# Raw input transposed first, and copies given to whichever engine is free: a two-block transformer kernel on one core

## Chip, cores and metric

The kernel runs on one core of a Trainium2 chip. It computes the forward pass of two transformer blocks for one sequence of 256 tokens of width 1024, everything in float32. The metric is the device time of one execution in microseconds, taken as the median of three executions. The kernel before takes 878.27 us (878.02 to 880.94).

## What is computed

`x` is 256 x 1024. The first block normalises it, multiplies it with `w_in` (and, later, with the four merge gates), runs four kinds of attention on the pieces, merges them and adds a feed-forward layer with a short convolution; the second block has two more mixers, a cross attention and another feed-forward layer. The change touches the first lines of this, which in the reference are:

```python
def rms_norm(x, gain):
    y = x * lax.rsqrt(jnp.mean(x * x, axis=-1, keepdims=True) + 1e-6)
    return y * gain
...
h = rms_norm(x, norm_attn_pre)        # 256 x 1024
p = h @ w_in                          # split into latent, key, value and gate columns
g = sigmoid(h @ w_merge_gate[j])      # four of them
```

The norm's factor is one number per token, so `(r * (x * gain)) @ w` equals `r * ((x * gain) @ w)`: it may be multiplied in on either side of the product.

## The kernel before

**Products.** Each float32 operand is split in two rounded parts, `hi` and `lo`, and a product is three TensorE products (hi times hi, hi times lo, lo times hi) that add up in one PSUM bank. `W` (line 439) does it for weights: a DMA into one of three `raw` buffers, a cast to `hi` on ScalarE (`S.copy`), a subtraction to `lo` on VectorE (`V.tensor_sub`). Activations are kept transposed: `XT` (line 457) holds, for each of eight slices of 128 of the 1024 inner columns, the `hi` and `lo` part of a 128 x 256 tile. `lin` (line 557) keeps activations stationary and streams up to 512 weight columns; `linT` (line 584) keeps weights stationary and streams 512 columns (both halves of the activation) or 256 (one half), by turns. There are 82 calls of `linT`, with sixteen products each.

**The start.** `mats1` (line 680) loads `x` in four pieces of 128 x 512 into `xs[0]` and `xs[1]` (`tt` is the half of 128 tokens), the first panel `wi0` of 432 columns in four pieces, and a constant table. For each half it forms the mean square (a square on ScalarE for one 512 columns, a square with sum on VectorE for the other), raises it to the power -0.5 on GpSimd, multiplies `x` by the factor on VectorE (line 711), and only then transposes it on TensorE (line 714) in eight pieces of 128 x 128. Each piece is copied out of PSUM with the gain, `hi` by ScalarE (`S.mul`, line 718) and `lo` by VectorE (line 719). The first product follows, `wi0`; its results go through `evac0`.

**The order of work.** No instruction is issued where it is written. `Plan` (line 21) records all of them, with what each reads and writes, and `trial` (line 160) plays them through with a cost per instruction (`_Op`, line 325): each engine takes, when it is free, the ready instruction with the lowest priority number for which a buffer is free. `hurry` (line 271) brings forward what TensorE waited for in the trial, and `issue` (line 291) keeps the best of 40 such rounds. The queues are then issued in that order, so the engines run their instructions strictly one after the other in an order fixed beforehand. Every instruction has a fixed engine: `S` is ScalarE, `V` VectorE, `G` GpSimd, `PE` TensorE; the author chose, line by line, which copies ScalarE makes and which VectorE.

**Places named later.** `attend` (line 646) computes two heads of an attention: scores, exponentials on ScalarE, four multiplications by the reciprocal sum, transposes by `transP` (line 628), values. `make_ffn` (line 1195) is the feed-forward layer: `natural` steps use `lin` and transpose the result back, `stationary` steps use `linT` and add the halves, `S.copy(u, acc[:, 0])` (line 1224). Since all instructions are issued from the recording layer, the profile shows them with line 101; the names of the tiles tell them apart: `bank` is a PSUM bank, `raw`, `hi`, `lo` the weights, `x` the activations in two parts and the input, `k` work tiles, `sm` small columns, `junk` a target that nobody reads, `ident` the identity matrix of the transposes.

## Time and profile before

| | us |
|---|---|
| median of three executions | 878.27 |
| the profiled execution | 878.73 |
| its span | 877.0 |
| TensorE busy | 858.2 |
| VectorE busy | 639.8 |
| ScalarE busy | 490.9 |
| GpSimd busy | 47.3 |

The profile shows one execution. The span runs from the first instruction to the last; 1.73 us of the execution's time lie outside it. A matmul's busy time is longer than the distance to the next one, because matmuls are pipelined: how fast TensorE goes is read from the distances between starts, not from the durations.

### The profile page before, as it was taken

How to read it: one execution, taken by the hardware profiler on the slowest of the kernel's cores; microseconds unless marked ns; L12 is line 12 of the kernel's file. 1: busy time of each engine (PE TensorE's matmuls, PEld its weight loads, DVE VectorE, ACT ScalarE, POOL GpSimd, SP SyncE). 2: the span in 40 equal slices, each digit the busy share in tenths (PEclk: the TensorE clock that was granted, in tenths of full speed). 3: DMA queues.
4: the chain of work that ended last, by engine and by line, in shares of the span. 5: the costliest groups of instructions: out<-in, count | busy, mean ns of one | idle time of the engine just before them, and what ended most of it. 6: DMA issues, size and time to landing. Idle time of an engine off the chain costs nothing.

```text
span 877.0 us, 12151 instructions
## 1 busy us (share of the span) xinstructions
PE 858.2 (98%) x4436; PEld 715.8 (82%) x4436; DVE 639.8 (73%) x1148; ACT 490.9 (56%) x845; POOL 47.3 (5%) x58
## 2 busy tenths in 40 slices
PE   6999999999999999999999999999999999999997
PEld 5779886778887888888888887788888888888886
DVE  6885648976667988888978677967855677666662
ACT  5675535654455667666654457656644555545441
POOL 1200000000001000000010111201100000000000
PEclk9999999999999999999999999999999999999999
DMA  7646653577456567665636564455633566656541
GB/s 246 213 148 201 210 178 97 178 215 220 133 175 218 171 212 223 207 194 180 205 131 201 173 191 146 144 169 168 202 111 97 186 201 215 213 182 200 182 134 49
DMA packets 45186, 156.08 MB, mean 178 GB/s; under 512 B 5263, under 2 KB 6841, under 8 KB 44997
## 3 DMA queue, kind: packets, MB, share of 16 engines
q1 hardware_dynamic: 44228, 153.10, 55.6%
q0 software_dynamic: 896, 2.19, 0.9%
q8 instruction: 35, 0.57, 0.3%
q14 instruction: 27, 0.21, 0.1%
HBM read 154.21 MB, written 1.06 MB: 177 GB/s over the span
## 4 chain that ended last, share of the span: by engine, by line
PE 82%; DVE 7%; ACT 4%; issue 2%; DMA 2%; POOL 1%; SPq 0%; DVEq 0%; POOLq 0%; ACTq 0%
PE bank L101 82%; DVE k L101 3%; ACT k L101 2%; DVE lo L101 2%; ACT hi L101 1%; DVE x L101 1%; POOL sm L101 1%; DMA raw<-in_fdn 1%; DVE sm L101 1%; DMA raw<-in_xkv 1%; DMA raw<-in_wi 1%; ACT junk L101 0%; ACT L101 0%; SPq L101 0%; ACT x L101 0%
## 5 line engine op out<-in xcount | busy, mean ns | idle before, releaser
L101 PE MATMUL bank<-hi,x 128*128 128x512 f32 (+3 forms) x1556 | 494.8, 393 | 2.0 <-ACT x L101 1.0
L101 DVE TENSOR_TENSOR lo<-raw,hi 128x1024 fp32r<-128x1024 f32 (+2 forms) x279 | 334.8, 1209 | 93.1 <-ACT hi L101 91.0
L101 ACT CAST hi<-raw 128x1024 fp32r<-128x1024 f32 (+2 forms) x279 | 287.6, 1039 | 102.0 <-PE bank L101 48.9
L101 PEld LDWEIGHTS bank<-hi,x 128*128 128x128 f32 (+1 forms) x1556 | 290.4, 188 | 60.1 <-DVE x L101 2.8
L101 PE MATMUL bank<-lo,x 128*128 128x512 f32 (+3 forms) x786 | 307.6, 393 | 0.1
L101 PE MATMUL bank<-x,hi 128*128 128x512 f32 x656 | 228.5, 398 | 0.0
L101 PE MATMUL bank<-x,lo 128*128 128x256 f32 x656 | 170.9, 281 | 0.0
L101 PEld LDWEIGHTS bank<-lo,x 128*128 128x128 f32 (+1 forms) x786 | 147.3, 187 | 28.5 <-DVE lo L101 0.8
L101 PEld LDWEIGHTS bank<-x,hi 128*128 128x128 f32 x656 | 119.0, 188 | 22.8
L101 PEld LDWEIGHTS bank<-x,lo 128*128 128x128 f32 x656 | 123.8, 189 | 7.6
L101 ACT COPY k<-bank 128x256 f32<-128x256 f32 (+5 forms) x116 | 46.1, 399 | 91.9 <-PE bank L101 91.6
L101 PE MATMUL bank<-ident,k 128*128 128x128 f32 (+2 forms) x362 | 58.5, 278 | 11.4 <-DVE k L101 9.8
L101 PEld LDWEIGHTS bank<-ident,k 128*128 128x128 f32 (+2 forms) x362 | 44.2, 140 | 25.1 <-DVE k L101 15.6
L101 POOL TENSOR_TENSOR sm<-sm,nhalf 128x1 f32<-128x1 f32 (+3 forms) x36 | 37.6, 1046 | 500.4 <-DVE sm L101 457.5
L101 DVE TENSOR_TENSOR x<-bank,x 128x512 fp32r<-128x512 f32 (+4 forms) x62 | 36.3, 608 | 28.3 <-PE bank L101 21.1
L101 DVE TENSOR_TENSOR k<-k,bank 128x256 f32<-128x256 f32 (+1 forms) x78 | 32.6, 419 | 26.4 <-ACT k L101 25.6
L101 PE MATMUL bank<-k,k 64*128 64x256 f32 (+12 forms) x364 | 49.0, 325 | 0.7 <-DVE k L101 0.7
L101 ACT ACTIVATE k<-bank 128x512 f32<-128x512 f32 (+4 forms) x41 | 19.7, 483 | 49.9 <-PE bank L101 47.7
L101 PEld LDWEIGHTS bank<-k,k 64*128 64x128 f32 (+4 forms) x364 | 37.7, 176 | 10.8 <-issue 4.1
L101 ACT ACTIVATE k<-bank,sm 128x256 f32<-128x256 f32 (+1 forms) x42 | 22.6, 566 | 27.4 <-PE bank L101 19.9
L101 DVE SCALAR_TENSOR_TENSOR k<-k,convw,k 128x255 f32<-128x255 f32 x72 | 34.4, 480 | 4.1 <-ACT k L101 3.4
L101 ACT CAST x<-bank 128x512 fp32r<-128x512 f32 (+2 forms) x49 | 24.4, 515 | 17.9 <-PE bank L101 17.2
(97 smaller groups left out, 404.7 us busy)
## 6 DMA issues: line engine op xcount, KB each, us to landing
raw<-in_wi SPq DMA_DIRECT2D x42, 512.0 KB, 4.4
raw<-in_up SPq DMA_DIRECT2D x40, 512.0 KB, 4.2
raw<-in_fup SPq DMA_DIRECT2D x36, 512.0 KB, 4.3
raw<-in_wg SPq DMA_DIRECT2D x32, 512.0 KB, 4.3
raw<-in_fdn SPq DMA_DIRECT2D x22, 512.0 KB, 4.6
raw<-in_dn SPq DMA_DIRECT2D x22, 512.0 KB, 4.6
raw<-in_xkv SPq DMA_DIRECT2D x16, 512.0 KB, 4.1
raw<-in_wo SPq DMA_DIRECT2D x8, 512.0 KB, 4.3
```

The lines of the kernel that those rows point to most:

```text
L101: op = _Op(self, n, eng, lambda: getattr(target, name)(*map(self.place, a), **{x: self.place(y) for x, y in k.items()}), name, outs, ins, k)
```

## The change

It has four parts.

1. The input goes to TensorE as it arrives. The transposes read `x` itself (`turn_in`), and the copies out of PSUM multiply with the gain alone. The gain is loaded as eight rows and transposed on TensorE, in place of a column load. The norm's factor is computed beside this and kept in spare columns of `nhalf` (`rx`, with `rq8` and `rhalf` as its multiples); it is multiplied in where results of products with `h` leave PSUM, mostly as the scalar of a copy that was there before. For `wi5`, whose results lie transposed, it is needed along the row: two products of a matrix of ones with a diagonal matrix make `rT`, and six multiplications apply it. Six products of ones are issued at the very start, into a bank that nobody reads. The first piece of `wi0` comes in two halves, the second half of `x` behind the second piece, and the constant table after that. The products of `wi0` for both token halves run side by side in two banks.
2. `nc.any`, here `AN`, records a copy or a scaling with two ways, one for VectorE and one for ScalarE. `trial` puts it in both queues and the engine that comes to it first takes it. Copies of transposes, of attention outputs, of the feed-forward's halves and the scalings in `attend` use it.
3. `issue` makes 120 rounds, and `hurry` sometimes pushes what a later product waits for.
4. `linT` first runs seven products with `hi`, then the eight with `lo`, then the last with `hi`.

The convolution's weights move from a tile of their own to a work buffer. The core of the diff:

```diff
@@ -106,6 +107,11 @@
             op = old
         elif self.gluing:
             self.glued = op
+        if other:
+            e2, t2, n2, a2, k2 = other
+            alt = _Op(self, n, e2, lambda: getattr(t2, n2)(*map(self.place, a2), **k2), n2, outs, ins, k2)
+            op.ways = {eng: (op.cost, op.parts), e2: (alt.cost, alt.parts)}
+            op.eng = "ANY"
         op.urgent = self.urgent
         op.prio = n - self.urgent * self.URGE - (0 if self.bulk else self.bonus) if self.at is None or name != "dma_start" else self.at
...
 
     reserve = {"k4": 1, "x8": 2, "k2": 3, "x2": 2, "k1": 2, "sm": 4, "PS": 2}
 
@@ -369,6 +394,20 @@
         return lambda *a, **k: self._p.add(self._e, self._t, name, a, k)
 
 
+class _Any:
+
+
+    def __init__(self, plan, nc):
+        self._p, self._nc = plan, nc
+
+    def copy(self, o, a):
+        self._p.add("DVE", self._nc.vector, "tensor_copy", (o, a), {}, ("ACT", self._nc.scalar, "copy", (o, a), {}))
+
+    def scale(self, o, a, c):
+        self._p.add("DVE", self._nc.vector, "tensor_scalar", (o, a, c, None), {"op0": OP.mult},
+                    ("ACT", self._nc.scalar, "mul", (o, a, c), {}))
+
+
 def tile_two_blocks(tc, T, out, dbg=None):
...
@@ -589,13 +629,11 @@
         h3 = hi.rearrange("p (k n) -> p k n", k=8)
         l3 = lo.rearrange("p (k n) -> p k n", k=8)
         plan.bulk = True
+        for kt in range(7):
+            PE.matmul(acc.rearrange("p a t -> p (a t)"), h3[:, kt], xt.both(kt), start=kt == 0, stop=False)
         for kt in range(8):
-            low = lambda: PE.matmul(acc[:, 0], l3[:, kt], xt.sl(kt, 0, 256)[0], start=False, stop=False)
-            if kt == 7:
-                low()
-            PE.matmul(acc.rearrange("p a t -> p (a t)"), h3[:, kt], xt.both(kt), start=kt == 0, stop=kt == 7)
-            if kt < 7:
-                low()
+            PE.matmul(acc[:, 0], l3[:, kt], xt.sl(kt, 0, 256)[0], start=False, stop=False)
+        PE.matmul(acc.rearrange("p a t -> p (a t)"), h3[:, 7], xt.both(7), start=False, stop=True)
         plan.bulk = False
         return acc
...
@@ -625,13 +663,13 @@
...
-    def transP(s, eng):
+    def transP(s):
...
         pT = sb([128, 384], "k2", name="pT")
-        eng(pT, ps)
+        AN.copy(pT, ps)
         return pT
...
         for u in range(2):
             for tt in (1, 0):
-                V.tensor_scalar(ss[u][:, COLS[tt]], ss[u][:, COLS[tt]], rec[:, 2 * tt + u:2 * tt + u + 1], None, op0=OP.mult)
-        pts = [transP(s, (V.tensor_copy, S.copy)[u]) for u, s in enumerate(ss)]
+                AN.scale(ss[u][:, COLS[tt]], ss[u][:, COLS[tt]], rec[:, 2 * tt + u:2 * tt + u + 1])
+        pts = [transP(s) for s in ss]
         values(po, pts, vs, first, last)
 
     def outT(oT, i, po):
-        S.copy(oT[0][:, i], po)
+        AN.copy(oT[0][:, i], po)
         V.tensor_sub(oT[1][:, i], po, f(oT[0][:, i]))
...
@@ -691,72 +729,113 @@
     plan = g["plan"]
     plan.at = -4000
-    for i in range(2):
-        nc.sync.dma_start(xs[0][:, i * 512:(i + 1) * 512], T["x"][:128, i * 512:(i + 1) * 512])
+    plan.urgent = True
+    ones = keep([128, 128], "ones")
+    V.memset(ones, 1.0)
+    warm = psS([128, 128])
+    for i in range(6):
+        PE.matmul(warm, ones, ones, start=True, stop=True)
+    h = XT(8)
+    chunks = two(T["wi0"])
+    first = []
...
+    def turn_in(tt, i):
+        tp = psS([128, 4, 128])
+        for j in range(4):
+            PE.transpose(tp[:, j, :], xs[tt][:, i * 512 + j * 128:i * 512 + (j + 1) * 128], ident)
+        for j in range(4):
+            k = 4 * i + j
+            hh, hl = h.sl(k, tt * 128, tt * 128 + 128)
+            S.mul(hh, tp[:, j, :], gcol[:, k:k + 1])
+            V.scalar_tensor_tensor(hl, tp[:, j, :], gcol[:, k:k + 1], f(hh), op0=OP.mult, op1=OP.subtract)
+
+    grow = sb([8, 128], "k1", name="grow")
+    nc.scalar.dma_start(grow, T["grow"])
+    load(0)
...
+    gp = psS([128, 8])
+    PE.transpose(gp, grow, ident[:8, :8])
+    V.tensor_copy(gcol, gp)
+    turn_in(0, 0)
+    first = [(W(chunks[0][0][:, j * 432:(j + 1) * 432], 432), 1) for j in range(2)]
+    turn_in(0, 1)
+    first.append((W(chunks[1][0], 864), 2))
+    load(1)
+    turn_in(1, 0)
+    first.append((W(chunks[2][0], 864), 2))
+    turn_in(1, 1)
+    first.append((W(chunks[3][0], 864), 2))
...
+    rcol = g["nhalf"][:, 8:14].rearrange("p (t c) -> p t c", t=2)
+    rx, rq8, rhalf = ([rcol[:, tt, i:i + 1] for tt in range(2)] for i in range(3))
...
     for tt in range(2):
-        r = g["rs2"](g["halves"](xs[tt], True))
-        for i in range(2):
...
-                PE.transpose(tp[:, j, :], xn[:, j * 128:(j + 1) * 128], ident)
-            for j in range(4):
-                k = 4 * i + j
-                hh, hl = h.sl(k, tt * 128, tt * 128 + 128)
-                S.mul(hh, tp[:, j, :], gcol[:, k:k + 1])
-                V.scalar_tensor_tensor(hl, tp[:, j, :], gcol[:, k:k + 1], f(hh), op0=OP.mult, op1=OP.subtract)
+        V.tensor_copy(rx[tt], g["rs2"](g["halves"](xs[tt], True)))
+        V.tensor_scalar(rq8[tt], rx[tt], -0.125, None, op0=OP.mult)
+        V.tensor_scalar(rhalf[tt], rx[tt], 0.5, None, op0=OP.mult)
+        V.tensor_scalar(dg[tt], ident, rx[tt], None, op0=OP.mult)
+        PE.matmul(rrow[:, tt * 128:tt * 128 + 128], ones, dg[tt], start=True, stop=True)
+    V.tensor_copy(rT, rrow)
 
     latg = sb([128, 384], "k2", name="latg")
...
+        S.mul(q[:, :, :64], a[:, 0], rq8[tt])
+        V.tensor_scalar(k[:, :, :64], a[:, 1], rx[tt], None, op0=OP.mult)
         cum = cps[:, tt, :]
         V.tensor_scalar(q[:, :, 64], cum, -1.0, None, op0=OP.mult)
...
     for c in range(6):
         acc = linT(h, T["wi5"][c], psA)
+        t = sb([128, 256], "k1", name="bqk")
         if c < 3:
-            t = sb([128, 256], "k1", name="bqs")
             S.mul(t, acc[:, 0], -0.125)
-            V.scalar_tensor_tensor(bq[:, c], acc[:, 1], -0.125, t, op0=OP.mult, op1=OP.add)
+            V.scalar_tensor_tensor(t, acc[:, 1], -0.125, t, op0=OP.mult, op1=OP.add)
         else:
-            t = sb([128, 256], "k1", name="bks")
             S.copy(t, acc[:, 0])
-            V.tensor_add(bk[:, c - 3], acc[:, 1], t)
-
+            V.tensor_add(t, acc[:, 1], t)
+        V.tensor_mul((bq if c < 3 else bk)[:, c % 3], t, rT)
 
     mg = [sb([128, 2, 512], "k4", name="merged") for _ in range(2)]
...
                 nat = sb([128, 512], "k2", name="nat")
-                S.copy(nat[:, :256], acc[:, :256])
-                V.tensor_copy(nat[:, 256:], acc[:, 256:])
+                AN.copy(nat[:, :256], acc[:, :256])
+                AN.copy(nat[:, 256:], acc[:, 256:])
                 u = us[c // 2][:, c % 2]
-                S.copy(u, acc[:, 0])
+                AN.copy(u, acc[:, 0])
                 V.tensor_add(u, u, acc[:, 1])
```

What the order becomes is shown at three places. ScalarE at the start, before: `x0` and `x1` are the halves of the input, `raw0` to `raw2` the pieces of `wi0`, `x80` and `x81` the transposed activations, `bank` tiles the transposes.

```order
L101 ACTIVATE junk0_133,sm1_120<-x0_150 128x512
L101 CAST hi0_66<-raw0_63 128x864
L101 CAST hi1_67<-raw1_64 128x864
L101 ACTIVATE x80_90<-bank0_135,sm0_119 128x128 x2
L101 CAST hi2_68<-raw2_65 128x864
L101 ACTIVATE x80_90<-bank0_135,sm0_119 128x128 x2
L101 ACTIVATE x81_91<-bank1_136,sm0_119 128x128 x4
L101 ACTIVATE junk0_133,sm3_122<-x1_151 128x512
L101 CAST hi3_69<-raw0_63 128x864
L101 CAST hi4_70<-raw1_64 128x1024
L101 ACTIVATE x80_90<-bank3_138,sm0_119 128x128 x4
L101 ACTIVATE x81_91<-bank4_139,sm0_119 128x128 x4
```

and now:

```order
L102 ACTIVATE junk0_133,sm1_120<-x0_150 128x512
L102 ACTIVATE x80_90<-bank2_137,sm0_119 128x128 x3
L102 CAST hi0_66<-raw0_63 128x432
L102 ACTIVATE x80_90<-bank2_137,sm0_119 128x128
L102 CAST hi1_67<-raw1_64 128x432
L102 ACTIVATE x81_91<-bank3_138,sm0_119 128x128 x4
L102 CAST hi2_68<-raw2_65 128x864
L102 ACTIVATE junk0_133,sm4_123<-x1_151 128x512
L102 ACTIVATE x80_90<-bank5_140,sm0_119 128x128 x4
L102 ACTIVATE x81_91<-bank6_141,sm0_119 128x128 x4
L102 CAST hi3_69<-raw0_63 128x864
L102 CAST hi4_70<-raw1_64 128x864
```

The gain copies of the first half (`x80`, `x81`) stand ahead of the first casts where they stood behind two of them, and the casts of half pieces (128x432) between them; no factor is waited for.

TensorE at the start, before (`k26`, `k27` are the normalised input):

```order
L101 MATMUL bank0_135<-ident_143,k26_100 128x128 x4
L101 MATMUL bank1_136<-ident_143,k27_101 128x128 x4
L101 MATMUL bank2_137<-hi0_66,x80_90 128x432
L101 MATMUL bank2_137<-lo0_74,x80_90 128x432
L101 MATMUL bank2_137<-hi0_66,x80_90 128x432 x2
L101 MATMUL bank2_137<-lo0_74,x80_90 128x432
L101 MATMUL bank2_137<-hi0_66,x80_90 128x432
L101 MATMUL bank2_137<-hi1_67,x80_90 128x432
```

and now:

```order
L102 MATMUL bank0_135<-ones_152 128x128 x6
L102 MATMUL bank1_136<-ident_143,k10_110 128x8
L102 MATMUL bank2_137<-ident_143,x0_150 128x128 x4
L102 MATMUL bank3_138<-ident_143,x0_150 128x128 x4
L102 MATMUL bank4_139<-hi0_66,x80_90 128x432
L102 MATMUL bank4_139<-lo0_74,x80_90 128x432
L102 MATMUL bank4_139<-hi0_66,x80_90 128x432
L102 MATMUL bank4_139<-hi1_67,x80_90 128x432
L102 MATMUL bank4_139<-lo1_75,x80_90 128x432
L102 MATMUL bank4_139<-hi1_67,x80_90 128x432
L102 MATMUL bank5_140<-ident_143,x1_151 128x128 x4
L102 MATMUL bank4_139<-hi2_68,x80_90 128x432
```

Ahead of the transposes stand six products of ones and the transpose of the gain; the transposes read `x0`, and those of the second half follow the products of the first two inner slices.

ScalarE at the first two up steps of the first feed-forward layer, before (`convw` is the convolution's weights, `k27` a result on its way to TensorE's transposes):

```order
L101 COPY k26_100<-bank7_142 128x256
L101 CAST hi2_68<-raw1_64 128x1024
L101 ACTIVATE k22_96<-bank4_139,convw_154 128x256 x2
L101 ACTIVATE k23_97<-bank0_135,convw_154 128x256 x2
L101 COPY k27_101<-bank1_136 128x256
L101 CAST hi6_72<-raw2_65 128x1024
```

and now (`k10` holds the convolution's weights; `k25`, `k20` belong to the first step, `k26` to the second):

```order
L112 COPY k25_99<-bank1_136 128x256 x2
L102 CAST hi0_66<-raw2_65 128x1024
L102 CAST hi3_69<-raw0_63 128x1024
L102 CAST hi2_68<-raw1_64 128x1024
L112 COPY k20_94<-bank3_138 128x256
L102 CAST hi5_71<-raw2_65 128x1024
L102 ACTIVATE k24_98<-bank5_140,k10_110 128x256 x2
L102 ACTIVATE k21_95<-bank4_139,k10_110 128x256 x2
L112 COPY k26_100<-bank7_142 128x256 x2
L102 CAST hi1_67<-raw0_63 128x1024
```

The copies of the first step are now shared with VectorE; the copy for the second step, now both halves of it, still stands behind four convolution instructions.

## Rows read from the trace of the kernel before

**Rows 1.** The page's first part: busy us, share, instructions.
```profile
PE 858.2 (98%) x4436; PEld 715.8 (82%) x4436; DVE 639.8 (73%) x1148; ACT 490.9 (56%) x845; POOL 47.3 (5%) x58
```

**Rows 2.** By stretch: busy (instructions) of PE, PEld, DVE, ACT, POOL; PEclk, DMA.
```profile
7.08:17.20 10.12, 8.64 (x24) 6.64 (x25) 7.78 (x17) 7.37 (x15) 2.32 (x4) 1.00 0.82 275
17.20:25.80 8.60, 8.60 (x47) 7.74 (x46) 6.50 (x22) 6.00 (x17) 1.11 (x2) 1.00 0.59 156
285.00:450.00 165.00, 165.00 (x863) 140.48 (x863) 144.03 (x225) 107.31 (x169) 1.54 (x2) 1.00 0.60 188
```

**Rows 3.** Timeline of the first 14 us: start, duration, instruction [idle before <-releaser].
```profile
3.68 0.63 ACT L101 ACTIVATE junk<-x 128x512 bf16<-128x512 f32 x1 [1.66 <-DMA x<-in_x]
7.08 1.97 PE L101 MATMUL bank<-ident,k 128*128 128x128 f32 x8 [7.08 <-DVE k L101]
10.00 0.73 PE L101 MATMUL bank<-hi,x 128*128 128x432 f32 x1 [0.96 <-ACT x L101]
13.10 1.09 PE L101 MATMUL bank<-hi,x 128*128 128x432 f32 x2 [0.52 <-DVE x L101]
```

**Rows 4.** Timeline, 14 to 26 us: the first product and the second half's transposes.
```profile
15.43 0.92 PE L101 MATMUL bank<-hi,x 128*128 128x432 f32 x2
16.51 0.92 PE L101 MATMUL bank<-hi,x 128*128 128x432 f32 x2
17.92 1.04 PE L101 MATMUL bank<-ident,k 128*128 128x128 f32 x8
18.56 2.17 ACT L101 ACTIVATE x<-bank,sm 128x128 fp32r<-128x128 f32 x8 [2.48 <-PE bank L101]
22.04 0.56 PE L101 MATMUL bank<-hi,x 128*128 128x432 f32 x2
22.63 0.55 PE L101 MATMUL bank<-hi,x 128*128 128x432 f32 x2
25.37 0.59 PE L101 MATMUL bank<-hi,x 128*128 128x432 f32 x2
```

**Rows 5.** ScalarE's groups by shape: count | busy us, mean ns | idle before.
```profile
L101 ACT COPY k<-bank 128x256 f32<-128x256 f32 x91 | 33.7, 371 | 76.6 <-PE bank L101 76.4
L101 ACT ACTIVATE junk<-x 128x512 bf16<-128x512 f32 x18 | 11.4, 632 | 30.1 <-DVE x L101 28.4 <-DMA x<-in_x 1.7
L101 ACT CAST hi<-raw 128x864 fp32r<-128x864 f32 x4 | 3.7, 916 | 3.5 <-DMA raw<-in_wi 3.5
```

**Rows 6.** VectorE's groups by shape.
```profile
L101 DVE COPY k<-bank 128x256 f32<-128x256 f32 x10 | 4.2, 422 | 3.6 <-ACT k L101 2.5 <-PE bank L101 1.0
L101 DVE TENSOR_TENSOR lo<-raw,hi 128x864 fp32r<-128x864 f32 x4 | 4.2, 1054 | 1.2 <-ACT hi L101 1.2
L101 DVE TENSOR_SCALAR k<-k,sm 128x256 f32<-128x256 f32 x34 | 11.7, 349 | 0.4
L101 DVE SCALAR_TENSOR_TENSOR x<-bank,sm,x 128x128 fp32r<-128x128 f32 x16 | 4.6, 344 | 2.0 <-ACT x L101 2.0
```

**Rows 7.** Timeline, 330 to 333 us: TensorE in two calls of linT.
```profile
331.95 0.40 PE L101 MATMUL bank<-x,hi 128*128 128x512 f32 x1
332.18 0.28 PE L101 MATMUL bank<-x,lo 128*128 128x256 f32 x1
332.30 0.40 PE L101 MATMUL bank<-x,hi 128*128 128x512 f32 x1
```

**Rows 8.** TensorE's waits: waited for: us in total, times, longest us.
```profile
PE bank L101 <- DVE k L101: 10.5, 9, 7.1
PE bank L101 <- ACT k L101: 1.3, 1, 1.3
```

**Rows 9.** Timeline, 281 to 285 us: the second up step's copy.
```profile
282.29 1.93 ACT L101 ACTIVATE k<-bank,convw 128x256 f32<-128x256 f32 x4
284.53 0.44 PE L101 MATMUL bank<-ident,k 128*128 128x128 f32 x2 [1.26 <-ACT k L101]
```

More of the change, by code (lines that the diff above doesn't have):

```diff
@@ L195, in trial @@
                 _, n = heapq.heappop(pend)
-                heapq.heappush(heaps[ops[n].eng], (prio[n], n))
+                for e in ("DVE", "ACT") if ops[n].eng == "ANY" else (ops[n].eng,):
+                    heapq.heappush(heaps[e], (prio[n], n))
+                    look[e] = True
             while rel and rel[0][0] <= t:
@@ L247, in trial @@
                 else:
-                    end = tfree[e] = t + o.cost
+                    end = tfree[e] = t + cost
                 done += 1
@@ L693, in mats1 @@
     plan.at = -4000
-    for i in range(2):
-        nc.sync.dma_start(xs[0][:, i * 512:(i + 1) * 512], T["x"][:128, i * 512:(i + 1) * 512])
-    gcol = small(8)
-    nc.sync.dma_start(gcol, T["gcol"])
-    first = two(T["wi0"])
-    for i in range(3):
-        first[i] = (W(first[i][0], 864), 2)
-    for i in range(2):
-        nc.sync.dma_start(xs[1][:, i * 512:(i + 1) * 512], T["x"][128:, i * 512:(i + 1) * 512])
-    first[3] = (W(first[3][0], 864), 2)
-    nc.sync.dma_start(g["cst"], T["cst"])
@@ new lines, in mats1, with load @@
+    ones = keep([128, 128], "ones")
[6 more added lines that the diff above has]
+    first = []
+    def load(tt):
+        for i in range(2):
+            c = slice(i * 512, (i + 1) * 512)
+            nc.sync.dma_start(xs[tt][:, c], T["x"][tt * 128:tt * 128 + 128, c])
+    def turn_in(tt, i):
[7 more added lines that the diff above has]
+            V.scalar_tensor_tensor(hl, tp[:, j, :], gcol[:, k:k + 1], f(hh), op0=OP.mult, op1=OP.subtract)
@@ L755, in evac0 @@
         hh = lat[0][:, :, tt * 128:(tt + 1) * 128]
-        S.copy(hh, tp)
+        AN.copy(hh, tp)
         V.tensor_sub(lat[1][:, :, tt * 128:(tt + 1) * 128], tp, f(hh))
-    lin(h, [(first, 432)], evac0)
+    accs = [psA([128, 432]) for _ in range(2)]
+    kt = 0
+    plan.bulk = True
+    for (hi, lo), kc in first:
+        h3, l3 = (w.rearrange("p (k n) -> p k n", k=kc) for w in (hi, lo))
+        for j in range(kc):
+            for tt in range(2):
+                mm3(accs[tt], *h.sl(kt, tt * 128, tt * 128 + 128), h3[:, j], l3[:, j], kt == 0, kt == 7)
+            kt += 1
+    plan.bulk = False
+    nc.sync.dma_start(g["cst"], T["cst"])
+    for tt in range(2):
+        evac0(0, tt, accs[tt])
     tab = sb([36, 16], "sm", name="tab")
@@ L860, in mats1 @@
                 PE.transpose(tp[:96, i, :], src[:, i, :], ident)
[L861 to L864 removed]
+            AN.copy(dst[:96, :, c0:c1], tp[:96])
     oTs = {}
@@ L1326, in trans4 @@
         if scale is None:
-            S.copy(d, tp)
+            AN.copy(d, tp)
         else:
```

135 lines of the change are left out of this document (73 added, 62 removed).

## The prediction

> **What bounds the kernel now.** The page's busy times come first: TensorE is busy for 858.2 of 877.0 us [rows 1], so the kernel is almost a single row of products, and an edit is worth only what it takes from TensorE's row or from the places where that row stands still. I then read TensorE's waits by cause [rows 8]. The named ones come to 10.5 + 1.3 = 11.8 us. One of them is 7.1 us, and the timeline shows that it is the start: the first eight transposes begin at 7.08, released by VectorE's normalised input, although the first half of `x` was there at 3.68, when ScalarE's square began [rows 3]. That leaves 11.8 - 7.1 = 4.7 us for all other named waits, in some ten places; the longest is 1.26 us, at the second up step of the first feed-forward layer, where a copy stands behind four convolution instructions on ScalarE [rows 9].
>
> The rest of the start is read from distances between products. The first product begins at 10.00; from 13.10 they follow without pause [rows 3]. From 15.43 to 16.51 three products start, 0.36 us each; from 22.04 to 22.63 three more, 0.197 each [rows 4]. The same 432 columns are streamed, so the early pace is that of 1.2 GHz and the late one that of 2.4, although the granted clock is printed as 1.00 in both stretches [rows 2]. The eight transposes tell the same: 1.97 us at 7.08, 1.04 us at 17.92 [rows 3, 4]. The change lies between 16.51 and 17.92. The last product of `wi0` ends at about 25.8; three products of `wi1` and two other transposes (0.9 us) were done between, so the net mark of the start is **24.9**. The same mark in the changed kernel gives the gain of the start.
>
> **The start in the changed kernel.** The transposes read `x`, so they go at 3.7 and fill the first bank after four at 0.25 us, at 4.7. What was waited for before, square, power and scaling, leaves the path. Next late is ScalarE, whose order the change section shows. After its square (3.68 + 0.63 [rows 3, 5] and the reading of its sum, so about 4.6) it has sixteen gain copies at 2.17/8 = 0.27 us [rows 4], together 4.35; two casts of half pieces at about 0.47 (half of the 0.916 [rows 5], an estimate), 0.94; three casts at 0.916, 2.75; and the second square, 0.8 with its sum. That is 8.85 us and ends at 13.5 to 14.0, if no load comes late. VectorE's two splits of the last pieces take 1.05 each [rows 6], the first from 13.1, so that the last `lo` is there at 15.2 to 15.6. Some twelve products stand behind that: 12 x 0.197 = 2.4.
>
> What TensorE does with this depends on its clock. Up to 12.5 it is limited by ScalarE's and VectorE's data: some 14 of the 48 products can have been done, 34 remain. At the fast pace from there the last data decide: 15.6 + 2.4 + two diagonal products at 0.13 to 0.25 (nearest: the transposes [rows 3, 4]) gives 18.4, a gain of 6.5. If the clock rises at 17.2, as now, 13 more products go by then at 0.36, and 21 at 0.197 take 4.1: 21.5, a gain of 3.4. At the slow pace throughout it would be 12.5 + 34 x 0.36 = 24.7, a gain of 0.2. I take a rise at about 15, because the row of products without pause, which now begins at 13.10, begins some 2 us earlier: 7 products by 15, then 27 x 0.197 = 5.3, so 20.3, and with the diagonal products 20.2 to 20.6. **The gain of the start is 4.5**, between 0.2 and 6.5.
>
> The six products of ones lie in the 3.7 us in which TensorE has nothing (6 x 0.25 = 1.5 us); they cost nothing, and whether they raise the clock is the difference between the cases above. The transpose of the gain stands ahead of the first transposes on TensorE: should the eight rows land after `x`, every transpose behind it waits, one for one. The diagonal products and the ready factor are not waited for before the results of `wi0` leave PSUM. Behind that, the products of `wi1` cover the additional multiplication of the two latent factors.
>
> **The factor at the exits.** Most of these multiplications are the scalar of a copy that is there anyway: nothing. The six with `rT` are new on VectorE, about 0.42 each by the copy of the same size [rows 6], 2.5 us, beside TensorE's products of `wi5` and the gates. Four scalings of the input (128 x 512) go. On the sum: 0.
>
> **`linT`.** The sixteen products stay, seven with `hi` in a row instead of by turns. A `hi` product takes 0.23 until the next start, a `lo` one 0.12 [rows 7], 8 x 0.35 = 2.8 us a call either way. If the order among them changed a distance by 0.01 us, 82 calls would make 82 x 0.01 = 0.8 either way. I take 0.
>
> **Copies by either engine, and more rounds.** By the new order VectorE has 26 more copies of 128 x 256, ScalarE as many fewer, 25 attention scalings went the other way, and eight `ah` scalings went to VectorE. A copy is dearer on VectorE, 0.422 against 0.371 [rows 5, 6]: 26 x 0.05 = 1.3 us more work, off the path. The Trainium skill ("VectorE: DVE Perf Modes", Specifications) states that VectorE lies closer to SBUF and ScalarE closer to PSUM, which speaks against moving copies out of PSUM to VectorE; the two rows agree with it, by 0.05 us a copy, and by it the sum stays as it is while VectorE has time to spare. What this part can win is bounded by the 4.7 us of named waits (with the small ones between them, little more); what it can lose has no row, so I set the same 4.7 on the other side. The longest wait seems to stay: in the new order both copies of the second up step still stand behind four convolution instructions on ScalarE, and then 1.26 + 0.37 could be waited for. I take **+2.0**, under half of the bound.
>
> **The sum.** 4.5 + 2.0 = 6.5. The profiled execution took 878.73, span 877.0 and 1.73 beside it; the median is 0.46 lower. Taken from the median: 878.27 - 6.5 = **871.8 us**.
>
> **The rivals.** A gain or loss of 0.5%, 4.4 us, is about what can be told from no change here, so "faster" is under 873.9 and "slower" over 882.7.
>
> *The clock rises no earlier and the copies win nothing.* Speaking for it: at present the eight transposes and sixteen products up to 17.20 (24 instructions [rows 2]) go at the slow pace [rows 3, 4], and the changed kernel's TensorE has pauses until 12.5, too. Then the start gives 3.4 and the rest 0: 874.9. The change would not have done what its copies are for. The Trainium skill ("TensorE: Matmul & The Clock Gate", Part 4: PE-mode transpose) says that transposes do not bring the full clock since they do not count as activity in the way products do. The rows agree as far as they go, since the first eight did not raise it; by that rule the early transposes help nothing here, and the time is this 874.9.
>
> *Waits grow elsewhere.* The new order is fitted more closely to the planner's costs, with copies put where an engine should be free; where it is not, the queue behind the copy waits. If half to all of the 4.7 came on top: 878.3 - 4.5 + 2.4 to 4.7, so 876.2 to 878.5.
>
> *The first feed-forward layer turns to VectorE, and the kernel gets slower.* From 285 to 450 VectorE is busy 144.0 of 165 us, TensorE all of it [rows 2]. In some ten of the eleven steps that leaves 2.1 us a step. At 0.422 a copy it takes five more copies a step before VectorE sets the pace, and one work buffer fewer (the convolution's weights hold it) ties the engines closer. If each of ten steps then waited as the second does now, 1.26 us [rows 9], it would be 12.6 us: 871.8 + 12.6 = 884.4. Against it: the order gives VectorE there about nine copies in the layer, not five a step, so 3.8 us of 21 spare.
>
> *More than forecast.* The clock is up from the first products (6.5), and the shared copies take most of the 4.7: 867.5.
>
> **How the numbers follow.** Forecast, start 3.5 to 6 and waits 0 to 4, 869 to 874.5: 0.55. Clock late and nothing else, 874 to 876: 0.17. Waits grow, 876 to 879: 0.13. More, 866 to 869: 0.10. Slower, 884 and about: 0.05. The range reaches from the lower end of "more" to the middle of "waits grow": 866.0 to 877.5, some 0.85. Faster: 0.10 and all but a little of 0.55, so 0.62; slower 0.06; the rest, 0.32, within 0.5%.
>
> **What would show it.** First transposes of `x` near 3.7, or at the landing of the gain's rows if that is the later; first product near 6.1; the distance of products falling from 0.36 to 0.197 near 15; last product of `wi0` at 20 to 20.6 (18.4, 21.5 or 24.7 in the other cases). Named waits of TensorE without the first: under 4.7 us, with one of 1.3 to 1.6 left near the second up step. VectorE's share from 285 to 450 about 0.90; over 0.97 with TensorE waiting for it would be the slower case. Distances in `linT` of 0.23 and 0.12 as before. Wrong I would be, above all, if TensorE in the first 12 us waits for something that the trace of before cannot show, a load put off by the new order of the queues, or if attention's stalls move more than the named waits tell.

## The result and the profile after

The changed kernel takes 871.95 us (median of four, 871.84 to 872.43); the kernel before, executed beside it, 879.0 (four, 878.02 to 880.94). The ratio is 0.9919, 95% interval 0.9904 to 0.9934: 7.1 us faster. The profiled execution has a span of 870.2 us against 877.0. Two executions at a far lower mean granted clock are left out of all figures here and below: one of experiment 11 (1059 us, 0.75) and one of the kernel before beside experiments 6, 9 and 11 (950 us, 0.85).

The first part of the page of the changed kernel, to be held against [rows 1]:

```profile
PE 858.7 (99%) x4453; PEld 719.8 (83%) x4453; DVE 663.0 (76%) x1201; ACT 479.5 (55%) x810; POOL 45.3 (5%) x58
```

TensorE is busy as long as before in a shorter span, and its share of the chain of work that ended last (part 4 of the page) goes from 82% to 89%. VectorE has 23 us more, ScalarE 11 less. TensorE's waits by cause in the changed kernel (total, times, longest), beside [rows 8]:

```profile
PE bank L102 <- DVE lo L102: 2.2, 3, 1.0
PE bank L102 <- DVE x L102: 1.4, 2, 0.8
PE bank L102 <- DVE ones L102: 1.1, 1, 1.1
PE bank L102 <- ACT hi L102: 0.8, 1, 0.8
PE bank L102 <- DVE k L102: 0.7, 2, 0.4
PE bank L102 <- ACT k L112: 0.6, 1, 0.6
PE bank L102 <- DVE sm L102: 0.3, 1, 0.3
```

The 7.1 us for the normalised input are gone; the first engine to be waited for is now VectorE with the matrix of ones, 1.1 us.

**Where the lead arises.** The two kernels stream the same columns in their three-part products, in a different order. I counted these columns through the starts of all products in a trace and read the time at which a given share of them has been started. The difference to the kernel before at the same share is the lead (worked out from the traces, us, one execution each):

| share started | 1/60 | 3/60 | 11/60 | 19/60 | 31/60 | 47/60 | last product |
|---|---|---|---|---|---|---|---|
| where | first of `wi1` | attention | after attention | first feed-forward | its end | second feed-forward | |
| before, time | 28.20 | 72.88 | 197.19 | 304.74 | 458.73 | 707.69 | 872.11 |
| changed, lead | 3.20 | 4.39 | 4.05 | 4.84 | 5.38 | 5.28 | 6.24 |

Half of it is the start. The rest grows in small amounts, also through the two feed-forward layers, where neither kernel has waits to lose. Another 0.6 of the 6.8 us between the spans lies behind the last product, in the landing of the output.

The old start varies more between executions than the new one. Experiment 1 below has the start of the kernel before, instruction for instruction, and its trace comes to 1/60 1.21 us later than the trace of before (first transposes at 7.38 instead of 7.08, fast pace only after 19 us). Experiment 2 has the start of the changed kernel and comes there at the same time to 0.01 us. So the 3.2 us of the start would be 4.4 against that other execution.

TensorE at the start of the changed kernel (start, duration, instruction, idle time before), beside [rows 3, 4]:

```profile
1.06 2.93 PE L102 MATMUL bank<-ones 128*128 128x128 f32 x12 [1.06 <-DVE ones L102]
...
4.12 1.75 PE L102 MATMUL bank<-ident,x 128*128 128x128 f32 x8
6.65 0.47 PE L102 MATMUL bank<-hi,x 128*128 128x432 f32 x1 [0.78 <-ACT hi L102]
7.75 0.46 PE L102 MATMUL bank<-lo,x 128*128 128x432 f32 x1 [0.64 <-DVE lo L102]
...
12.59 0.76 PE L102 MATMUL bank<-hi,x 128*128 128x432 f32 x3
13.19 0.36 PE L102 MATMUL bank<-lo,x 128*128 128x432 f32 x1
...
16.57 0.66 PE L102 MATMUL bank<-lo,x 128*128 128x432 f32 x2 [0.59 <-DVE lo L102]
...
21.00 0.59 PE L102 MATMUL bank<-hi,x 128*128 128x432 f32 x2
```

The first transposes stand at 4.12 instead of 7.08 and the first product at 6.65 instead of 10.00. From 12.59 to 13.19 three products start, 0.2 us each: the pace of 2.4 GHz, which came after 16.5 before. At 16.57 TensorE has waited for the `lo` part of the third piece; the last product of `wi0` ends at 21.4, where the net mark before was 24.9. ScalarE's list is late, too:

```profile
5.27 0.88 ACT L102 ACTIVATE x<-bank,sm 128x128 fp32r<-128x128 f32 x3 [0.98 <-PE bank L102]
...
7.09 0.37 ACT L102 ACTIVATE x<-bank,sm 128x128 fp32r<-128x128 f32 x1 [0.50 <-DVE x L102]
...
11.86 1.14 ACT L102 ACTIVATE x<-bank,sm 128x128 fp32r<-128x128 f32 x4 [0.65 <-DVE x L102]
13.43 0.37 ACT L102 ACTIVATE x<-bank,sm 128x128 fp32r<-128x128 f32 x1 [0.42 <-DVE x L102]
14.35 0.92 ACT L102 CAST hi<-raw 128x864 fp32r<-128x864 f32 x1 [0.55 <-DMA raw<-in_wi]
15.59 0.91 ACT L102 CAST hi<-raw 128x864 fp32r<-128x864 f32 x1 [0.32 <-DMA raw<-in_wi]
```

Its list ends at 16.50, not at 13.5: it begins 0.57 us later than at 4.7, waits 1.57 us for VectorE between gain copies, and 0.87 for the loads of the third and fourth piece. SyncE issued the third at 7.72: the two halves of the first piece and the second piece held all three `raw` buffers. The `lo` parts themselves are VectorE's work:

```profile
14.61 0.68 DVE L102 CUSTOM_DVE_ANT_0 k<-x 128x512 f32<-128x512 f32 x1
...
15.47 2.12 DVE L102 TENSOR_TENSOR lo<-raw,hi 128x864 fp32r<-128x864 f32 x2
```

The split of the third piece begins at 15.47, as soon as VectorE is through with its gain parts and its second square, which wait for no load of `wi0`. ScalarE's cast of that piece had ended at 15.27.

### The profile page after: what moved, and what is told of

It reads as the page before. It is cut to its first block, busy times and chain, and to the rows that moved or that the text cites. A ratio compares the mean times of both kernels' runs of the same rounds, so it can differ in the third digit from the quotient of the medians.

```text
span 870.2 us, 12251 instructions
## 1 busy us (share of the span) xinstructions
PE 858.7 (99%) x4453; PEld 719.8 (83%) x4453; DVE 663.0 (76%) x1201; ACT 479.5 (55%) x810; POOL 45.3 (5%) x58
## 4 chain that ended last, share of the span: by engine, by line
PE 89%; DVE 5%; issue 2%; ACT 1%; DMA 1%; POOL 1%; DVEq 0%; POOLq 0%; ACTq 0%
PE bank L102 89%; DVE k L102 2%; DVE lo L102 1%; DVE x L102 1%; POOL sm L102 1%; DMA raw<-in_fdn 1%; DMA raw<-in_fupn 1%; ACT x L102 0%; DVE sm L102 0%; ACT junk L102 0%; ACT k L102 0%; ACT hi L102 0%; ACT k L112 0%; DVEq L1756 0%; ACT sm L102 0%
## 5 line engine op out<-in xcount | busy, mean ns | idle before, releaser
L102 DVE TENSOR_TENSOR lo<-raw,hi 128x1024 fp32r<-128x1024 f32 (+3 forms) x280 | 334.7, 1203 | 79.5 <-ACT hi L102 77.9
L102 ACT CAST hi<-raw 128x1024 fp32r<-128x1024 f32 (+3 forms) x280 | 288.7, 1036 | 140.2 <-PE bank L102 57.9
L102 PE MATMUL bank<-x,hi 128*128 128x512 f32 x656 | 167.9, 392 | 0.0
L102 PEld LDWEIGHTS bank<-x,lo 128*128 128x128 f32 x656 | 89.7, 190 | 6.5
L102 PE MATMUL bank<-x,lo 128*128 128x256 f32 x656 | 91.8, 282 | 0.0
L112 ACT COPY k<-bank 128x256 f32<-128x256 f32 (+3 forms) x78 | 31.1, 409 | 56.8 <-PE bank L102 52.3
L102 PE MATMUL bank<-ident,k 128*128 128x128 f32 (+3 forms) x347 | 53.3, 275 | 1.0 <-DVE k L102 0.7
L102 PEld LDWEIGHTS bank<-ident,k 128*128 128x128 f32 (+3 forms) x347 | 41.5, 138 | 13.8 <-DVE k L102 4.7
L102 PEld LDWEIGHTS bank<-k,k 64*128 64x128 f32 (+4 forms) x364 | 38.7, 176 | 11.5 <-issue 4.9
L102 DVE COPY k<-bank 128x256 f32<-128x256 f32 (+7 forms) x60 | 28.1, 473 | 22.3 <-PE bank L102 22.0
L102 DVE SCALAR_TENSOR_TENSOR k<-k,k,k 128x255 f32<-128x255 f32 x72 | 34.3, 479 | 1.5 <-ACT k L102 0.7
```

The costliest lines, as they stand in the source:

```text
L102: op = _Op(self, n, eng, lambda: getattr(target, name)(*map(self.place, a), **{x: self.place(y) for x, y in k.items()}), name, outs, ins, k)
L112: alt = _Op(self, n, e2, lambda: getattr(t2, n2)(*map(self.place, a2), **k2), n2, outs, ins, k2)
```

## Experiments

Each kernel was timed beside the kernel before. The medians of before in these comparisons lie between 878.1 and 879.0. Where only the order of emission is touched, the planned order is that of the kernel named, instruction for instruction, so that no other difference comes in.

**1 and 2. linT's order alone, in both directions.** After the planning, the sixteen products of every call change seats among themselves:

```diff
+        for grp in self.calls:
+            seats = sorted(seat[o.n] for o in grp)
+            for i, o in zip(seats, [grp[j] for j in (0, 2, 4, 6, 8, 10, 12, 1, 3, 5, 7, 9, 11, 13, 14, 15)]):
+                turn[i] = o.n
```

In the kernel before, into the new order:

> The kernel before, its plan untouched; only the sixteen products of each linT call change seats among themselves, into the new order (seven hi, eight lo, one hi). Theory A: the order itself is worth about 0.02 us a call, because in the changed kernel TensorE's lead over before grows slowly through stretches of linT (5.28 us at the 694th us, 6.24 at the last product): 82 x 0.02 = 1.7, so about 876.6, with hi-to-hi 0.228 and lo-to-lo 0.120 where hi-to-lo was 0.235. Rival B (the prediction): a product takes its time whatever follows: 878.3 within 0.3.

In the changed kernel, back into the old order:

> The changed kernel, its plan untouched; the sixteen products of each linT call go back to the old order by turns. Theory A: 1.7 us slower than the changed kernel, 873.6. Rival B: 871.9 within 0.3.

Measured: 876.14 us (ratio 0.9976, 0.9967 to 0.9986), 2.3 faster than before; and 874.07, 2.1 slower than the changed kernel. In the traces the lead over the unaltered kernel grows from -1.21 (1/60) to 1.14 (last product), 2.35 us, and falls from 0.00 to -2.15. Theory A holds in both directions, and the effect is larger than the 1.7 expected. TensorE in the kernel before with the new order, at the same place as [rows 7]:

```profile
330.98 1.11 PE L102 MATMUL bank<-x,lo 128*128 128x256 f32 x8
331.93 2.00 PE L102 MATMUL bank<-x,hi 128*128 128x512 f32 x8
333.77 1.12 PE L102 MATMUL bank<-x,lo 128*128 128x256 f32 x8
```

Eight `lo` take 0.95 (0.119 each) and eight `hi` 1.84 (0.230 each): 2.79 a call. By turns it is 0.23 to 0.24 behind a `hi` and 0.12 behind a `lo`; over all pairs of the trace the medians are 0.235 and 0.118, against 0.228 and 0.120 in rows of one kind. All distances within and between calls add up to 225.6 us in the kernel before and to 223.3 with the new order (worked out from the starts in the two traces): 0.02 to 0.04 us a call, too little to see in two rows, and 82 times it is two microseconds. Why the distances differ is not shown. It is not the next product alone: by turns a `hi` at the end of a call, followed by another `hi`, takes 0.234, too (63 places), and in the new order the `hi` ahead of the first `lo` takes 0.227 (81 places).

**3. Without the products of ones.** The six products are planned but not emitted.

> The changed kernel, its plan untouched, without the six products of ones at the start. Theory A: they are why the pace was 0.2 us a product from 12.3 us on where it rose at about 17 before; without them the clock rises 2 to 3 us later, some 7 to 10 products at 0.36 instead of 0.2, 1.1 to 1.6 us, about 873.2. Rival B: the products and transposes of the real work raise the clock as early: 871.9, full pace from 12.3.

Measured: 871.72 us (871.38 to 872.2), the changed kernel's 871.95 within its spread. Rival B holds for the time; the pace is another matter. The granted clock of both (from:to, length, PE busy, PEclk, DMA share, GB/s), first the changed kernel:

```profile
9.00:10.00 1.00, 1.00 (x7) 0.50 0.96 268
...
12.00:13.00 1.00, 1.00 (x6) 0.84 0.80 272
```

and without the ones:

```profile
9.00:10.00 1.00, 1.00 (x7) 1.00 0.97 367
```

TensorE without the ones:

```profile
3.66 1.97 PE L103 MATMUL bank<-ident,x 128*128 128x128 f32 x8 [0.34 <-DMA x<-in_x]
...
11.73 0.75 PE L103 MATMUL bank<-hi,x 128*128 128x432 f32 x3
12.32 0.36 PE L103 MATMUL bank<-lo,x 128*128 128x432 f32 x1
...
16.35 0.66 PE L103 MATMUL bank<-lo,x 128*128 128x432 f32 x2 [1.26 <-DVE lo L103]
```

With the ones the eight transposes took 1.75 us instead of 1.97, so the clock rose within them. Then TensorE stood still for 0.78 and 0.64 us, and the granted clock is 0.50 from 9 to about 12.3, the level of 1.2 GHz. Without them the transposes begin 0.46 earlier, the products are at 0.2 us by 11.7, before those of the kernel with the ones, and what that wins is lost again in the wait for the third piece: 1.26 us instead of 0.59, ending at 16.35 instead of 16.57.

That is one execution of each, and the clock is not the same in all. Experiment 2 has the same order up to its first call of `linT`, ones included. In its trace TensorE pauses likewise (0.56 and 0.63 us), but the granted clock stays up; the wait for the third piece ends where it ended in the changed kernel, and the lead over that kernel at 1/60 is 0.00:

```profile
9.00:10.00 1.00, 0.90 (x7) 1.00 0.86 246
...
16.57 0.66 PE L103 MATMUL bank<-lo,x 128*128 128x432 f32 x2 [0.72 <-DVE lo L103]
```

So the clock ahead of 12 us does not decide the end of `wi0` in these orders; the split of the third piece does. What holds that split back can be read without the ones as well. ScalarE and VectorE there:

```profile
13.47 1.72 ACT L103 CAST hi<-raw 128x864 fp32r<-128x864 f32 x2
...
15.25 2.02 DVE L103 TENSOR_TENSOR lo<-raw,hi 128x864 fp32r<-128x864 f32 x2
```

The third piece landed at 11.79 here, and ScalarE's casts wait for no load. The split still begins at 15.25, because it stands behind VectorE's gain parts and second square in the order, and `wi0` ends at 21.2. It is the order of VectorE's list that sets this end, not the landing.

**4. The new start alone.** Engines fixed as before, old search, `linT` by turns.

> The changed kernel with its new start alone: engines fixed as before, the old search of 40 rounds, linT by turns. Theory A (the parts add up): the start is worth 3.5 us, as the trace shows at the end of wi0 (21.4 against 24.9): 874.8. Rival B: a new order of the plan costs or wins some 2 us by luck, so 872.8 or 876.8, with waits in attention or the first feed-forward layer that neither kernel has. Rival C: the start needs the longer search, so that its gain is under 2 us: over 876.3.

Measured: 878.05 us (ratio 0.9995, 0.9986 to 1.0003): no gain at all. The trace shows which rival. The issues of loads on SyncE, those on GpSimd, and TensorE:

```profile
0.74 0.38 SPq L102 DMA_DIRECT2D raw<-in_wi  x1
1.18 0.89 SPq L102 DMA_DIRECT2D x<-in_x  x2
...
1.28 0.71 POOL L102 DMA_DIRECT2D k<-in_mla_q_norm  x1 [0.34 <-issue]
...
8.30 1.11 PE L102 MATMUL bank<-ident,x 128*128 128x128 f32 x4 [3.50 <-DMA x<-in_x]
```

The old search had brought a piece of `wi0` ahead of `x`, and GpSimd's broadcast load, issued at 8.07 in the changed kernel, stands at 1.28. The second 512 columns of `x` landed at 8.26 instead of 4.40, and TensorE waited 3.5 us. Which of the two loads held it is not separated; the first 512 columns, behind the piece of `wi0` alone, still landed at 3.90. The lead is 0.41 at 1/60. Rival C: the start hangs on the search.

**5. The changed kernel with the old search** (40 rounds, old `hurry`).

> The changed kernel with the old search: 40 rounds and the old rule for what is brought forward, which may move the first loads too. Theory A: the gain of the start hangs on the order of the first loads. In the run with the new start alone the second 512 columns of x landed at 8.26 instead of 4.40, behind a piece of wi0 and GpSimd's broadcast loads, and the lead at the first products of wi1 was 0.4 us instead of 3.2. With the old search this comes back here: some 3 us slower than the changed kernel, 874.5 to 875.5. Rival B: the old search costs under 1 us, and the missing gain of the start alone lay with the fixed engines: 872 to 873.

Measured: 877.91 us (ratio 0.9991, 0.9982 to 0.9999). The same wait, 3.7 us for `x`, stands in its waits, and the lead is 0.80 at 1/60. It costs more than theory A said, 6 us: through attention the lead falls to -0.36 at 11/60, so this order is also worse behind the start. One searched order does not tell whether the shared copies are why.

**6. The start alone with the first loads kept in order**: experiment 4 with one condition more in the old `hurry`. The new `hurry` of the changed kernel has this condition, too: it brings none of the first loads forward, which part 3 in the list of the change leaves out.

```diff
-                    if start[n] - ready[n] > 50.0:
+                    if start[n] - ready[n] > 50.0 and not (ops[n].dma and ops[n].prio < -1000):
                         new[n] -= push
```

> The run with the new start alone, with one line more: the old search of 40 rounds may not bring forward the first loads. Theory A: the order of the first loads is what the start hung on; x lands whole at 4.4 as in the changed kernel, wi0 ends near 21.4, and the kernel is 3 us faster than the start alone: 874.5 to 875.5. Rival B: the loads are in order, but the old search leaves new waits elsewhere, as the one after the shared copies did: lead of 3 us at the first products of wi1, and 876.5 to 878 at the end. Rival C: the loads are not it: no lead at wi1.

Measured: 876.65 us (ratio 0.9977, 0.9966 to 0.9988). The order of the loads is the cause, as far as the start goes: `x` lands at 4.40, and the lead is 2.83 at 1/60, 3.55 at 3/60. But rival B holds at the end. At 11/60 the lead is 0.66. TensorE's waits in the attention stretch between, with the bracket that names them:

```profile
138.91 0.87 PE L102 MATMUL bank<-k,k 128*64 128x128 f32 x8 [0.99 <-DVE k L102]
140.50 0.88 PE L102 MATMUL bank<-ident,k 128*128 128x128 f32 x6 [0.72 <-DVE k L102]
...
169.80 0.33 PE L102 MATMUL bank<-ident,k 128*128 128x128 f32 x1 [0.80 <-DVE k L102]
```

With three shorter ones, some 3.7 us of named waits stand there. The changed kernel has two in this stretch:

```profile
154.44 0.30 PE L102 MATMUL bank<-hi,x 128*60 128x256 f32 x1 [0.82 <-DVE x L102]
160.66 0.50 PE L102 MATMUL bank<-lo,x 128*128 128x512 f32 x1 [0.95 <-DVE lo L102]
```

The microseconds won at the start stay only as long as the order behind it is as good as before.

**7. Fixed engines in the changed kernel.** New start, new search, `linT` as changed; every shared copy on its engine of before.

> The changed kernel with every shared copy and scaling back on its engine of before; start, new search and linT as changed. Theory A: first loads in order, so the start keeps its 3.3 and linT its 2.2; the shared copies were worth about 1 us: 872.5 to 873.5. Rival B: without shared copies the start falls back as in the run with the start alone: 875.5 to 876.5.

Measured: 873.89 us (873.6 to 875.34), 1.9 slower than the changed kernel. The start is kept (lead 3.53 at 1/60), so theory A's first half holds; the size is twice that expected. One wait of TensorE stands out:

```profile
156.75 0.30 PE L102 MATMUL bank<-hi,x 128*60 128x256 f32 x1 [3.73 <-DVE x L102]
```

At this place the changed kernel waits 0.82. Behind the pause the granted clock is 0.51 from 157.6 to 161.0, half speed. The lead, level with the changed kernel's at 3/60, is 2.8 us behind it at 11/60. Later stretches win 1.3 of that back.

**8 and 9. Everything but the start, with and without the shared copies.** Both have the old start, the new search and `linT`'s new order.

> The kernel before with everything but the start: shared copies, new search, linT's order. Theory A (the parts add): 871.95 + 3.3 = 875.2, of which linT is 2.2 and the copies and the search 1. Rival B: the copies and the search win nothing of their own: 876.2. Rival C: they won most, and the start little: 873.

> The kernel before with the new search of 120 rounds and linT's order; engines fixed, start as before. It splits the 1.85 us by which the run without the new start (874.29) is faster than linT's order alone (876.14). Theory A: the shared copies are worth it: 876.0. Rival B: the longer search is: 874.5. Between seeds 0.9 us are chance, so a value from 874.8 to 875.6 would settle nothing.

Measured: 874.29 us with the copies (ratio 0.9944, 0.9932 to 0.9956), 875.17 without (0.9961, 0.9947 to 0.9975). The first lies between theory A and rival C: by it the start is worth 2.3 us. The second lies where its expectation says that it settles nothing. Taken as they are, with 876.14 for `linT`'s order alone, the search is worth 1.0 and the copies 0.9 here, and the copies 1.9 in experiment 7.

**10. Another seed.**

> The changed kernel with another seed of the search's random choices, nothing else. It shows how much of the difference between two searched orders is chance. Theory A: under 1 us, 871.0 to 873.0. Rival B: 2 us or more, 870 or 874; then no part whose order was searched anew can be priced by its median alone.

Measured: 872.83 us (872.47 to 873.98), 0.9 slower than the changed kernel. So theory A holds: 0.9 us between two searched orders can be chance, and the split of experiments 7 to 9 is no better than that: search and copies together won 1 to 3 us, and which of them more stays open.

**11 and 12. A better start.** No products of ones, and both halves of the first piece in one `raw` buffer, with seed 17 and with the changed kernel's own seed.

```diff
-    first = [(W(chunks[0][0][:, j * 432:(j + 1) * 432], 432), 1) for j in range(2)]
+    raw = sb([128, 864], "raw", name="raw")
+    whi = sb([128, 864], "hi", F32R, name="whi")
+    wlo = sb([128, 864], "lo", F32R, name="wlo")
+    for j in range(2):
+        c = slice(j * 432, (j + 1) * 432)
+        nc.sync.dma_start(raw[:, c], chunks[0][0][:, c])
+        S.copy(whi[:, c], raw[:, c])
+        V.tensor_sub(wlo[:, c], raw[:, c], f(whi[:, c]))
+    first = [((whi, wlo), 2)]
```

> The changed kernel without the products of ones and with both halves of the first piece of wi0 in one raw buffer (and hi and lo likewise), so that the third piece need not wait for a buffer: it was issued at 7.72 and landed at 14.32, and its lo part came at 16.57, when TensorE had waited 0.8 us. The seed of the search is 17. Theory A: the third piece lands before 11.5, the wait in wi0 goes, wi0 ends 0.8 to 1.5 us earlier, and with the search's luck 870.0 to 871.0. Rival B: VectorE's and ScalarE's lists end no earlier (second square and sixteen gain copies stand ahead), so wi0 ends as before: 871.5 to 872.5.

> The same edit of the start (no products of ones, one raw buffer for the first piece's halves) with the changed kernel's own seed, 1. The run with seed 17 was 2.85 us faster than the changed kernel, with a lead of 1.45 us over it at the first products of wi1 and 3.4 from the attention stretch on. Theory A: the edit of the start is worth 0.9 to 1.5 us of this and the rest was the search's luck: wi0 ends near 20.5 again, 870.4 to 871.1. Rival B: it is all the edit, since what the search did later follows from it: 869.0. Rival C: all luck, wi0 ends at 21.4: 871.9.

Measured: 868.1 to 869.4 us with seed 17 (ratio 0.9885, 0.987 to 0.9901) and 868.91 with seed 1 (0.9893, 0.9877 to 0.991), some 3 us faster than the changed kernel and the fastest of all. ScalarE, VectorE, SyncE and TensorE at seed 1:

```profile
12.09 0.91 ACT L102 CAST hi<-raw 128x864 fp32r<-128x864 f32 x1
13.13 0.88 ACT L102 ACTIVATE x<-bank,sm 128x128 fp32r<-128x128 f32 x3
13.90 0.92 ACT L102 CAST hi<-raw 128x864 fp32r<-128x864 f32 x1
...
13.62 1.05 DVE L102 TENSOR_TENSOR lo<-raw,hi 128x864 fp32r<-128x864 f32 x1
...
4.03 0.43 SPq L102 DMA_DIRECT2D raw<-in_wi  x1
...
19.64 0.59 PE L102 MATMUL bank<-hi,x 128*128 128x432 f32 x2
```

The third piece is issued at 4.03 instead of 7.72, its cast stands at 12.09 with no wait for a load, and `wi0` ends at 20.1 instead of 21.4. The order is another: the cast and the split of the third piece now stand ahead of the last three gain copies on either engine. The split begins 1.85 us earlier (13.62 for 15.47), and the lead over the changed kernel is 1.87 us at 1/60; at 11/60 it is 3.06. That the planner moved them because it could count on an earlier landing is likely, but not tested by itself, and the missing ones are part of the edit.

So theory A names the mechanism, but its 0.9 to 1.5 is too small, and 868.91 is the time of rival B, "all the edit". The 1.2 us that arise between 1/60 and 11/60 belong to an order searched anew. Luck alone explains little of the whole: both seeds gain there (2.0 with seed 17), and two orders with the edit (medians 868.91 and 868.78) lie 3 us and more below two without it (871.95 and 872.83).

## Why the prediction was right, and where it was not

The time, 871.8 forecast and 871.95 measured, came out through errors that cancel: the start and the copies gave less than forecast, `linT` gave what was put at nothing. That the two times agree to 0.15 us is luck.

**`linT`, forecast 0, measured 2.1 to 2.3.** This is the term that was mis-sized. The prediction read two distances to 0.01 us from [rows 7] and bounded the effect by 0.01 us a call. But a call has sixteen distances, and seven pairs of them change partner: a difference of 0.003 to 0.005 us in each pair, below what the rows print, makes 0.02 to 0.035 a call and 1.7 to 2.9 us over 82 calls. A bound for a repeated edit has to be worked out from the sum of a whole call: 2.81 to 2.83 between the calls' pairs of `lo` before (at 330.79, 333.60 and 336.43), 2.79 after.

**The start, forecast 4.5, measured 3.2 to 3.5** in the traces of before and after (2.3 by the time of experiment 8, 4.4 against the trace of experiment 1). The path was right: the transposes at the landing of `x`, ScalarE's and VectorE's lists next, and the full pace came at 12.6, earlier than the 15 that was taken. With that pace alone the sum would have ended near 18.4; it ended at 21.4. That is the mark that the prediction had set for a late clock (21.5), reached for another reason. The step that failed is the two lists, added up as if neither engine ever waited for the other: ScalarE's to 13.5 to 14.0 and VectorE's last two splits from 13.1. ScalarE began 0.57 us later and waited 1.57 for VectorE between the gain copies and 0.87 for two loads behind a buffer that the halves of the first piece had taken, 3.0 us in all. VectorE began the splits at 15.47, behind gain parts that wait for ScalarE's in turn and behind its second square, which the prediction had not put on VectorE's list. By the run without the ones the loads are not what held the first split: it began at 15.25 there without a wait for one.

The prediction counted the casts of the two halves but not the buffer that each of them holds. In experiment 12, with one buffer and another order, ScalarE's list ends at 14.8 and `wi0` at 20.1, where the prediction had put it (20.2 to 20.6). There, too, two errors cancel: the list ends later than 14.0 and the full pace comes at 11.5 instead of 15.

**Copies and search, forecast 2.0, measured about 1.** From 6.24 us of lead at the last product, 3.2 are the start and 2.15 `linT`: 0.9 are left, within chance by experiment 10. The 4.7 us of named waits in the prediction leave out two lines of the view of [rows 8]:

```profile
PE bank L101 <- ACT x L101: 1.0, 1, 1.0
PE bank L101 <- DVE x L101: 0.9, 2, 0.5
```

Of these, 1.5 us lie in the start and 0.4 behind it, so that 5.1 us were there to be won behind `wi0`. In the changed kernel TensorE's named waits there sum up to 4.0: lo 1.0, x 1.4, k 0.7 and 0.6, sm 0.3. Only 1.1 went. The one that was to stay is gone; at the second up step ScalarE and TensorE show

```profile
277.57 1.92 ACT L102 ACTIVATE k<-bank,k 128x256 f32<-128x256 f32 x4
279.38 0.66 ACT L112 COPY k<-bank 128x256 f32<-128x256 f32 x2
...
279.35 0.39 PE L102 MATMUL bank<-lo,x 128*128 128x512 f32 x1
279.81 0.71 PE L102 MATMUL bank<-ident,k 128*128 128x128 f32 x4
```

The copies stand behind the four convolution instructions, as the order said; but these begin 2 us ahead of the end of TensorE's products, where in [rows 9] they began 1.0 ahead (282.29 against 284.53 - 1.26) and the wait was 1.26. Now it is 0.2. From the order alone the wait could not be told.

**The rest.** The six products of ones were to take 1.5 us and cost nothing. The trace shows them as twelve records of 2.93 us together, up to 3.99; they put the transposes off by 0.46 us (3.66 without, 4.12 with them), behind a wait that hid it. VectorE's share of the first feed-forward layer was forecast as 0.90; the changed kernel's row (as in [rows 2]) says 149.04 of 165. TensorE does not wait there (busy for 164.98), so the slower rival did not come. Nor did the late clock: the pace rose at 12.6, and without the ones before 11.8. The end of `wi0` did not hang on the clock in these orders (experiment 3). The rule of the Trainium skill that belongs to it ("TensorE: Matmul & The Clock Gate", Part 4: PE-mode transpose, by which transposes do not bring the full clock) stays open: without the ones the first eight, 1.97 us, brought no fast pace (a product of 432 columns still took 0.36 us from 7.8 on), and no run here has more transposes alone ahead of the products.

The rival in which waits grow elsewhere came with other search settings (experiments 5, 6 and 7), not with these. That the start would bring nothing without the new search, none of the rivals had foreseen; the prediction's last sentence names the place, "a load put off by the new order of the queues". Part 3 of the change, priced at a share of 2 us, carries part 1, by the one condition that keeps the first loads in their places.

## What to carry to other kernels

Where a planner sets the order, price an edit with its order and not by itself: here the same start was worth 0.4 or 2.8 us at its own end, by whether the first loads kept their places (experiments 4 and 6), and searched orders of one program differ by 0.9. In the list of what is next late, follow both engines that feed each other, with all that stands in their queues, and count the buffers that an edit takes as well as its instructions: a piece that comes in two halves held two. And for an edit repeated a thousand times, add up whole repetitions from the trace before calling it nothing.

## What the runs showed of the hardware

By turns with products of 256 columns, a product of 512 columns starts its successor after 0.235 us (median of the kernel before), in rows of its own kind after 0.228 (experiment 1). The 256-column ones go the other way by 0.002 (0.118 by turns, 0.120 in rows). The kind of the next product alone does not set this, as experiment 1 says. Grouping them was worth 2.1 to 2.3 us of 878.

One order of instructions does not fix the clock of the first microseconds. In the profiled execution of the changed kernel the clock that the products of ones had raised was back at 0.50 when the real ones ran, after two pauses of 0.78 and 0.64 us; in that of experiment 2, with the same order and pauses of 0.56 and 0.63, it stayed up. Of seven traces with the ones, five have the full clock by 6.3 us (the eight transposes take 1.09 us in experiment 7 and 1.22 in 10); four of these five are at 0.50 by 9 us. The other two have the slow pace until 13.4 (1.97 for the eight transposes in experiment 6). Of the three traces of the new start without the ones, none has the full clock before 10.4.

The granted clock of the first microseconds has to be read with the distances: the view says 1.00 until 8 us with the ones and throughout without them, while 432 columns still take 0.36 us there at 8 us. The trace of before lists no level at all ahead of 17.44 us, where the pace rises, and the view prints 1.00 where none is listed.
